# Weight sums in halves, a moved filler unit, a pinned opening and a later transpose in a two-layer decoder trunk

## The chip, the cores and the metric

The kernel runs on one core of one Trainium2 chip (trn2). The metric is the device time of one execution in microseconds (us); lower is better. Engines are named as in the profile: PE is TensorE's matmul side and PEld its weight load, DVE is VectorE, ACT is ScalarE, POOL is GpSimd, SP is SyncE, which here only issues DMAs.

## The reference

Two decoder layers over 256 tokens of width 2048, everything in float32:

```
for i in range(2):
    h = rms_norm(x, attn_norm[i])
    x = x + (diff_attention(h) if i == 0 else mla_attention(h))
    x = x + memory_cross_attention(rms_norm(x, cross_norm[i]), mem_h)   # 256 memory tokens
    h = rms_norm(x, mlp_norm[i])
    x = x + square(relu(h @ mlp_wup[i])) @ mlp_wdown[i]                 # 2048 -> 8192 -> 2048
return rms_norm(x, final_norm)
```

Differential attention takes q, k and v from one 2048 x 6144 weight, rotates a part of each q and k head by position (RoPE), and takes the difference of two softmaxes. The layers' weights are about 0.5 GB in all, and each is read once.

## The kernel before

**Precision.** A float32 product is made of three products in a shorter format: each operand is split into a high part (a cast) and a low part (the value less its high part). For a weight tile `raw` of 128 x 2048, ScalarE casts `whi <- raw` (line 195) and VectorE subtracts `wlo <- raw, whi` (line 196), in pieces of 128 x 1024; a piece is called a half below. For each 128 rows TensorE runs activation-high x weight-high, activation-high x weight-low, activation-low x weight-high: the order matters, since the second of the three is the first that needs `wlo`.

**Pipeline.** A weight unit is one `raw` tile of 1 MB, loaded by a DMA on SP's queue. There are seven raw slots (`RAWS`), and four slots each for `whi` and `wlo`, of one half each. So ScalarE may cast a half as soon as TensorE is done with the half four before it, and VectorE must then have its low part ready when TensorE gets there. `take()` hands a unit to the matmul loops and `fill()` keeps four of them issued ahead. Just before `fill()` splits one job, it calls `begin()` of the job behind it.

**Orders.** TensorE's order is the program's own. A clock kept by the program (`clock[0]`, 0.2267 us for a product of 512 columns) decides when a side task (a transpose, a softmax) is put among the matmuls. The other engines' orders are worked out by a scheduler with its own time line, except where instructions carry an order token: those with one token stay in program order on their engine. All `wlo` subtractions and weight sums carry the token "weights" (`in_turn`).

**Seven products.** In the MLP's first matrix, and in three of the four column groups of the first layer's q and k (a subclass, `Chained`), a 2 x 2 block product is made with seven instead of eight products, p1 to p7 (`class Seven`, order p1, p5, p3, p7, p2, p6, p4). Each has two items x0 and x1 of 12 matmuls. p5 and p7 need sums of weight blocks. p5's is p1's tile plus another loaded block, and p7's is p3's tile plus the same block: a VectorE add of 128 x 2048 in place, issued in `begin()` (line 836; line 915 for `Chained`, p5 only). The sums for p6, p7 of `Chained` and p4 are made by accumulating DMAs on POOL's queue (line 839).

**The MLP line.** `mlp_line` interleaves the items: x0, x1, then one ordinary unit R of 24 matmuls, then the next product. p4 of one block runs after p1 of the next. There are seven such blocks in each of the two layers. Five ordinary units are left over, and each goes as a spare unit between x0 and x1 of p3, in blocks 2 to 6.

**The opening.** The first weight unit is loaded in four pieces of 512 columns (`split_pieces(first, 4 * CH, 4)`). The first activation unit is given transposed (`xT`), and is scaled by the norm's gains and split: ScalarE line 358 makes the high part of one 128 x 256 piece, VectorE line 359 the low part. In the program, a weight cast and an activation part alternate. TensorE runs 13 warm-up products on a blank tile meanwhile.

**The first queries.** `heads_T` evacuates q from its bank (line 522), POOL rotates it (lines 533 to 538, once for each 128 tokens, t = 0 and 1), and TensorE transposes the result (`flip`, line 159) `T_ROT + given_wait` = 24 us later by the program's clock, for both t.

Of the kernel before, what the change touches and what calls it, by code (L numbers as in the profile page):

```python
# [13 lines left out]
AF = mybir.ActivationFunctionType  # L14
ALU = mybir.AluOpType
# [6 lines left out]
CH = 512  # L22
# [23 lines left out]
def trunk(ctx, tc, x, xT, mem, memT, positions, gcols, gfinal, lam_vecs, consts, W, out):  # L46
    nc = tc.nc
# [15 lines left out]
    def nm(s):  # L63
        serial[0] += 1
        return f"{s}_{serial[0]}"

    def unit():
        return units.tile([P, 2, 4, S], F32R, tag="unit", name=nm("unit"))
# [10 lines left out]
    class Task:  # L79
        def __init__(self, gen):  # L80
            self.gen = gen
            self.done = False
            self.waits = None
            self.ready = clock[0]
            self.serial = serial[0]
            side.append(self)
            self.step()
# [53 lines left out]
    def side_bank():  # L141
        while not free_banks[0]:
            yield 0.5
        free_banks[0] -= 1
        return bank()
# [15 lines left out]
    def f32(ap):  # L161
        return ap.bitcast(F32)

    def load(dst, src, queue=None):
        tc.keep_in_program_order((queue or nc.sync).dma_start(dst, src))


    def in_turn(ins):
        tc.stamp_issue_order_token(ins.ins, "weights")
        return ins  # L170

    def raw_tile():
        return wraw.tile([P, 4 * CH], F32, tag="raw", name=nm("raw"))

    def split_weights(src, width, pieces=2, loads=1, queue=None):
# [4 lines left out]
            load(raw[:, i * m : (i + 1) * m], src[:, i * m : (i + 1) * m], queue)  # L180
        return halves_of(raw, n, pieces)

    class split_pieces:
        def __init__(self, raw, n, pieces):
            self.raw, self.n, self.m, self.i = raw, n, n // pieces, 0
            self.halves = []

        def next(self):
            m, i = self.m, self.i
            at = i * m % (self.n // 2)  # L190
            if at == 0:
                self.halves.append([whalf.tile([P, 2 * CH], F32R, tag=tag, name=nm(tag)) for tag in ("whi", "wlo")])
            hi, lo = (w[:, at : at + m] for w in self.halves[-1])
            r = self.raw[:, i * m : (i + 1) * m]
            nc.scalar.copy(hi, r)  # L195
            in_turn(nc.vector.tensor_tensor(lo, r, f32(hi), ALU.subtract))  # L196
            self.i += 1

    def halves_of(raw, n=4 * CH, pieces=2):
        split = split_pieces(raw, n, pieces)  # L200
        for _ in range(pieces):
            split.next()
        return split.halves
# [135 lines left out]
    def transpose4(src, pt):  # L339

        for k in range(4):
            flip(pt[:, k * P : (k + 1) * P], src[:, k * P : (k + 1) * P])
        return pt.rearrange("p (k t) -> p k t", k=4)

    def given_unit(src, u, gcol, pieces=None):


        dst = Held(unit())
        rows = raw_tile().rearrange("p (k t) -> p k t", t=S)
        for k, n in ((0, 1), (1, 1), (2, 2)) if pieces else ((0, 2), (2, 2)):  # L350
            load(rows[:, k : k + n], src[:, 4 * u + k : 4 * u + k + n, :])
            if pieces and k == 0:
                load(g, gcols)
            for i in range(k, k + n):
                if pieces:
                    pieces.next()
                raw, hi, gain = rows[:, i], dst[:, 0, i], g[:, gcol + 4 * u + i : gcol + 4 * u + i + 1]
                nc.scalar.activation(hi, raw, AF.Copy, scale=gain)  # L358
                nc.vector.scalar_tensor_tensor(dst[:, 1, i], raw, gain, f32(hi), ALU.mult, ALU.subtract)
        return dst  # L360

# [158 lines left out]
    def evacuate(ps, scale):  # L520
        e = work.tile([P, CH], F32, tag="ev", name=nm("ev"), bufs=EVS)
        nc.scalar.activation(e[:, : ps.shape[1]], ps, AF.Copy, scale=scale)
        return e
# [16 lines left out]
    def heads_T(ps, t, scale, dst, rot=None, spare=False, given=None, given_wait=0.0):  # L540


        def task():
            while given and not given():
                yield 0.5
            e = evacuate(ps, scale() if given else scale)
            if rot:
                cos, sin, heads, half = rot
                rope(e.rearrange("p (h d) -> p h d", h=heads), cos, sin, heads, half)
            yield T_ROT + given_wait if rot else T_EV  # L550
            b = ps
            if spare:
                b = yield from side_bank()
            split(dst, t, transpose4(e, b))
            if spare:
                give_back()
            yield T_TURN

        dst.run(task())
# [245 lines left out]
    class Seven:  # L805
# [20 lines left out]
        def begin(self, p, x):  # L826
            r, other = self.raw, None
            if p in self.B:
                r[p, x] = self.fetch(*self.B[p], x)
            elif p == "p5":  # L830
                r[p, x], other = r.pop(("p1", x)), self.fetch(0, 1, x)
                r["12", x] = other
            elif p == "p7":
                r[p, x], other = r.pop(("p3", x)), r.pop(("12", x))
            if other is not None:
                in_turn(nc.vector.tensor_tensor(r[p, x], r[p, x], other, ALU.add))  # L836

        def added(self, o, block, x):
            tc.keep_in_program_order(nc.gpsimd.dma_start(o, self.source(*block, x), accum_op=ALU.add))  # L839
# [67 lines left out]
    class Chained(Seven):  # L907

        def begin(self, p, x):
            r = self.raw  # L910
            if p in self.B:
                r[p, x] = self.fetch(*self.B[p], x)
            elif p == "p5":
                r[p, x], r["p7", x] = r["p1", x], self.fetch(0, 1, x)
                in_turn(nc.vector.tensor_tensor(r[p, x], r[p, x], r["p7", x], ALU.add))  # L915

        def spent(self, p, x):
            if p == "p5":
# [3 lines left out]
    def mlp_line(l):  # L922

        def up(b, h):
            return Chunk(l, "up", [(b, h)]).items()

        def both(b):
            return [(b, 1), (b, 0)] if b else [(b, 0), (b, 1)]  # L930

        opened = {}

        def down(b):
            shut, begun = ((0, 1), (2, 3)) if b % 2 else ((2, 3), (0, 1))
            line = []
            for c in shut:
                line += opened.pop(c)[2:] if c in opened else Chunk(l, "down", both(b), c).items()
            for c in begun:
                if b == MLP_BLOCKS - 1:  # L940
                    line += Chunk(l, "down", both(b), c).items()
                else:
                    opened[c] = Chunk(l, "down", both(b) + both(b + 1), c).items()
                    line += opened[c][:2]
            return line

        first, rest = up(0, 0) + up(0, 1), []
        for b in range(MLP_BLOCKS - 1):
            rest += down(b)
        line, rest = first[:6], first[6:] + rest  # L950
        pairs = []
        held = None
        for b in SEVEN:
            by = {p: [] for p in Seven.ORDER}
            for item in Seven(f"mlp_wup{l}", 2 * b, b).items():
                by[item.u[0]].append(item)
            for p in Seven.ORDER[:-1]:
                pairs.append((p, by[p]))
                if p == "p1" and held:
                    pairs.append(("p4", held))  # L960
            held = by["p4"]
        extra = len(rest) - len(pairs) - 5
        for n, (p, (x0, x1)) in enumerate(pairs):
            line.append(x0)
            if p == "p3" and extra > 0 and n > 6:
                line.append(rest.pop(0))
                extra -= 1
            line += [x1, rest.pop(0)]
        line += rest[:2] + held + rest[2:]
        return line, down(MLP_BLOCKS - 1)  # L970
# [58 lines left out]
    acts = []  # L1029
    norm = Stream(G_ATTN)  # L1030
    pieces = split_pieces(first, 4 * CH, 4)
    ready.append(pieces.halves)
    for u in range(4):
        acts.append(given_unit(xT, u, G_ATTN, pieces if u == 0 else None))
# [237 lines left out]
    da_scales = []  # L1272
# [16 lines left out]
    def rotation(t):  # L1289
        return cos[:, t, :hd], sin[:, t, :hd], 4, hd  # L1290
# [53 lines left out]
    for i, dst in enumerate((q, k)):  # L1344
        ps = matmul_chunk(acts)
        for t in range(NT):
            heads_T(ps[t], t, lambda i=i, t=t: da_scales[i][t], dst, rotation(t), given=lambda: da_scales, given_wait=8.0 if i else 12.0, spare=True)
    v, before, copied = [], None, {}
    free_banks[0] -= 1
    for gi, line in enumerate(diff_lines):  # L1350
        o = attend_group(q, k, v, 5.0)
        nq, nk, nv = Held(unit()), Held(unit()), []
        other = value_steps(v) if gi == 0 else output_steps(before)
# [13 lines left out]
    o = attend_group(q, k, v, 0.0)  # L1367
    m = []
# [46 lines left out]
    ps = matmul_chunk(acts, LAT)  # L1415
    latent_piece(eq, 0, ps, 0, LAT)
    ps = matmul_chunk(acts, LAT)
# [3 lines left out]
    ps = matmul_chunk(acts, 320)  # L1421
# [70 lines left out]
    norm, m, mk = attention(project_q, project_kv, attend_latent, G_CROSS + 16)  # L1492
# [114 lines left out]
```

## Time and profile before

| | before |
|---|---|
| median of 3 runs | 2219.71 us (2217.9 to 2219.93) |
| the profiled execution, own time | 2220.47 us |
| its span, first to last instruction | 2218.4 us |
| PE busy | 2199.4 us (99%), 10733 matmuls |
| PEld busy | 1849.9 us (83%) |
| DVE busy | 1750.3 us (79%) |
| ACT busy | 1405.0 us (63%) |
| POOL busy | 186.2 us (8%) |
| HBM read | 499.08 MB, 226 GB/s over the span |
| mean granted TensorE clock | 0.998 |

The profiled execution's own time is its span plus 2.07 us around it, and lies 0.76 us above the median of the runs. A timeline row gives the start of a group of instructions, the time it took, the engine, the line, the operation with its tiles (out <- in), the count, and in brackets how long the engine had been idle before and what ended that. A busy PE is not PE at its peak: a matmul's recorded duration overlaps the next, so PE's pace is read from the distance between the starts of its rows.

### The profile page before, as it was taken

The numbers are of one execution on the slowest core, as the hardware profiler recorded it, in microseconds if no ns is written. First come the engines' busy times: TensorE is split into PE (matmuls) and PEld (weight loads), VectorE is DVE, ScalarE is ACT, GpSimd is POOL, SyncE is SP. The second block draws the span as 40 slices with busy tenths as digits, with TensorE's granted clock in tenths as the row PEclk, the third lists the DMA queues.
The fourth block names the chain that finished last, engine by engine and source line by source line (L and its number), as shares of the span: only waits on it lengthen the run. The fifth ranks groups of instructions, "written<-read, shape, count | busy, mean of one in ns | idle before, by whom it ended". The sixth has DMA issues, their size and how long they took to land.

```text
span 2218.4 us, 28131 instructions
## 1 busy us (share of the span) xinstructions
PE 2199.4 (99%) x10733; PEld 1849.9 (83%) x10733; DVE 1750.3 (79%) x1939; ACT 1405.0 (63%) x1889; POOL 186.2 (8%) x268
## 2 busy tenths in 40 slices
PE   9999999999999999999999999999999999999998
PEld 7888888988888888888889998898888888888886
DVE  7988877778878878888765767778887887887874
ACT  7666677566666666656645654656666666666664
POOL 1221120000000000000000410000000000000001
PEclk9999999999999999999999999999999999999999
DMA  9779797345886886886945343734688678688691
GB/s 371 201 251 278 236 294 249 123 151 218 258 274 223 260 271 222 262 269 218 294 158 195 115 152 129 270 134 152 227 264 268 229 252 266 228 252 270 226 305 57
DMA packets 75447, 503.00 MB, mean 227 GB/s; under 512 B 8625, under 2 KB 9009, under 8 KB 17201
## 3 DMA queue, kind: packets, MB, share of 16 engines
q1 hardware_dynamic: 63504, 421.51, 50.9%
q0 software_dynamic: 10656, 77.60, 17.9%
q10 hardware_dynamic: 1152, 2.10, 0.3%
q8 instruction: 84, 1.38, 0.2%
q14 instruction: 51, 0.41, 0.0%
HBM read 499.08 MB, written 2.10 MB: 226 GB/s over the span
## 4 chain that ended last, share of the span: by engine, by line
PE 93%; DVE 4%; ACT 1%; issue 1%; POOL 0%; DMA 0%; ACTq 0%; POOLq 0%; DVEq 0%
PE mm L155 62%; PE pr L155 25%; PE ax L155 3%; PE ax L159 2%; DVE raw L836 2%; DVE wlo L196 2%; ACT whi L195 1%; PE mm L159 1%; DMA raw<-in_da_wqkv_dram 0%; DVE unit L332 0%; DVE unit L494 0%; DVE unit L432 0%; POOL rs L371 0%; POOL rope L533 0%; DVE raw L915 0%
## 5 line engine op out<-in xcount | busy, mean ns | idle before, releaser
L196 DVE TENSOR_TENSOR wlo<-raw,whi 128x1024 fp32r<-128x1024 f32 (+3 forms) x998 | 1198.8, 1214 | 392.4 <-ACT whi L195 359.2
L195 ACT CAST whi<-raw 128x1024 fp32r<-128x1024 f32 (+3 forms) x998 | 1038.2, 1042 | 693.0 <-PE mm L155 466.7
L155 PE MATMUL mm<-whi,unit 128*128 128x512 f32 (+2 forms) x3904 | 1241.3, 388 | 4.3 <-ACT unit L358 3.4
L155 PEld LDWEIGHTS mm<-whi,unit 128*128 128x128 f32 x3904 | 729.9, 188 | 145.9 <-ACT unit L358 4.2
L155 PE MATMUL mm<-wlo,unit 128*128 128x512 f32 (+2 forms) x1952 | 753.7, 386 | 2.8 <-DVE wlo L196 2.3
L155 PE MATMUL pr<-whi,unit 128*128 128x512 f32 x1904 | 610.9, 390 | 0.0
L155 PEld LDWEIGHTS mm<-wlo,unit 128*128 128x128 f32 x1952 | 367.6, 188 | 76.3 <-DVE wlo L196 9.9
L155 PEld LDWEIGHTS pr<-whi,unit 128*128 128x128 f32 x1904 | 357.5, 188 | 73.5
L155 PE MATMUL pr<-wlo,unit 128*128 128x512 f32 x952 | 370.6, 389 | 0.0
L155 PEld LDWEIGHTS pr<-wlo,unit 128*128 128x128 f32 x952 | 178.8, 188 | 36.2
L839 POOL DMA_DIRECT2D raw<-in_mlp_wup_dram x56 | 49.1, 877 | 1118.7 <-DVE wlo L196 997.4
L836 DVE TENSOR_TENSOR raw<-raw,raw 128x2048 f32<-128x2048 f32 x56 | 127.9, 2284 | 0.0
L517 DVE TENSOR_TENSOR x<-x,mm 128x512 f32<-128x512 f32 x152 | 99.7, 680 | 8.0 <-PE mm L155 7.9
L155 PE MATMUL mm<-unit,whi 128*128 128x256 f32 x512 | 93.0, 284 | 0.0
L155 PEld LDWEIGHTS mm<-unit,whi 128*128 128x128 f32 x512 | 80.2, 192 | 0.4
L371 POOL TENSOR_TENSOR rs<-rs,mhalf 128x1 f32<-128x1 f32 (+1 forms) x28 | 29.3, 1051 | 553.0 <-DVE rs L370 553.0
L155 PE MATMUL mm<-unit,wlo 128*128 128x256 f32 x256 | 72.4, 283 | 0.0
L331 ACT CAST unit<-ax 128x512 fp32r<-128x512 f32 (+1 forms) x88 | 49.3, 566 | 28.5 <-PE ax L159 25.3
L332 DVE TENSOR_TENSOR unit<-ax,unit 128x512 fp32r<-128x512 f32 (+1 forms) x88 | 57.7, 661 | 3.1
L155 PEld LDWEIGHTS mm<-unit,wlo 128*128 128x128 f32 x256 | 49.1, 192 | 0.0
L365 ACT ACTIVATE junk<-x 128x512 bf16<-128x512 f32 x56 | 35.2, 628 | 9.3 <-DVE x L517 8.3
L155 PE MATMUL ax<-unit,unit 128*128 128x256 f32 (+1 forms) x240 | 36.9, 280 | 0.0
(197 smaller groups left out, 1117.6 us busy)
## 6 DMA issues: line engine op xcount, KB each, us to landing
raw<-in_mlp_wup_dram SPq DMA_DIRECT2D x128, 1024.0 KB, 5.0
raw<-in_mlp_wdown_dram SPq DMA_DIRECT2D x128, 1024.0 KB, 6.4
raw<-in_mlp_wup_dram POOLq DMA_DIRECT2D x56, 1024.0 KB, 10.7
raw<-in_da_wqkv_dram SPq DMA_DIRECT2D x45, 1024.0 KB, 10.7
raw<-in_da_wqkv_dram POOLq DMA_DIRECT2D x18, 1024.0 KB, 11.8
raw<-in_da_wo_dram SPq DMA_DIRECT2D x16, 1024.0 KB, 10.7
raw<-in_ca_wkv_dram SPq DMA_DIRECT2D x16, 1024.0 KB, 5.0
raw<-in_mla_wo_dram SPq DMA_DIRECT2D x16, 1024.0 KB, 5.5
```

The lines of the kernel that those rows point to most:

```text
L155: return nc.tensor.matmul(o, stationary, moving, start=start, stop=stop, skip_group_check=not alone)
L159: nc.tensor.transpose(o, src, ident)
L195: nc.scalar.copy(hi, r)
L196: in_turn(nc.vector.tensor_tensor(lo, r, f32(hi), ALU.subtract))
L331: nc.scalar.copy(hi, src)
L332: nc.vector.tensor_tensor(dst[:, 1, :n, t * P : (t + 1) * P], src, f32(hi), ALU.subtract)
L365: nc.scalar.activation(junk[:, : src.shape[1]], src, AF.Square, accum_out=acc)
L371: nc.gpsimd.tensor_tensor(r[:, :n], r[:, :n], mhalf.broadcast_to([P, n]), ALU.pow)
L517: nc.vector.tensor_tensor(xc, xc, ps, ALU.add)
L836: in_turn(nc.vector.tensor_tensor(r[p, x], r[p, x], other, ALU.add))
L839: tc.keep_in_program_order(nc.gpsimd.dma_start(o, self.source(*block, x), accum_op=ALU.add))
```

## The change

Four edits:

1. A weight sum is no longer issued whole in `begin()`. `sum_between` puts it on a list, `between`, as two adds of 128 x 1024, and the next two calls of `split_pieces.next()` (any unit's) each issue one of them, after the cast and ahead of the low part. All carry the token "weights".
2. The spare unit in blocks 2 to 6 of the MLP line goes between x0 and x1 of p5, no longer of p3.
3. In the opening, the four casts of the first weight unit and the four high parts of the first activation unit carry a new token, "opening", so that ScalarE runs them as the program has them, in turn.
4. The wait of the first queries' transposes is 3 us longer for t = 1.

```diff
+    def opening(ins):
+        tc.stamp_issue_order_token(ins.ins, "opening")
...
+    between = []
+
+    def sum_between(o, other, n=2):
+
+        m = 4 * CH // n
+        for i in range(n):
+            at = slice(i * m, (i + 1) * m)
+            between.append(lambda at=at: in_turn(nc.vector.tensor_tensor(o[:, at], o[:, at], other[:, at], ALU.add)))
...
             self.halves = []
+            self.placed = None
...
-            nc.scalar.copy(hi, r)
+            cast = nc.scalar.copy(hi, r)
+            if self.placed:
+                self.placed(cast)
+            if between:
+                between.pop(0)()
             in_turn(nc.vector.tensor_tensor(lo, r, f32(hi), ALU.subtract))
...
-                nc.scalar.activation(hi, raw, AF.Copy, scale=gain)
+                part = nc.scalar.activation(hi, raw, AF.Copy, scale=gain)
+                if pieces:
+                    opening(part)
...
             if other is not None:
-                in_turn(nc.vector.tensor_tensor(r[p, x], r[p, x], other, ALU.add))
+                sum_between(r[p, x], other)
...
                 r[p, x], r["p7", x] = r["p1", x], self.fetch(0, 1, x)
-                in_turn(nc.vector.tensor_tensor(r[p, x], r[p, x], r["p7", x], ALU.add))
+                sum_between(r[p, x], r["p7", x])
...
-            if p == "p3" and extra > 0 and n > 6:
+            if p == "p5" and extra > 0 and n > 6:
...
     pieces = split_pieces(first, 4 * CH, 4)
+    pieces.placed = opening
...
-            heads_T(ps[t], t, ..., given_wait=8.0 if i else 12.0, spare=True)
+            heads_T(ps[t], t, ..., given_wait=8.0 if i else 12.0 + 3.0 * t, spare=True)
```

More of the change, by code (lines that the diff above doesn't have):

```diff
@@ L1346, in trunk @@
         for t in range(NT):
-            heads_T(ps[t], t, lambda i=i, t=t: da_scales[i][t], dst, rotation(t), given=lambda: da_scales, given_wait=8.0 if i else 12.0, spare=True)
+            heads_T(ps[t], t, lambda i=i, t=t: da_scales[i][t], dst, rotation(t), given=lambda: da_scales, given_wait=8.0 if i else 12.0 + 3.0 * t, spare=True)
     v, before, copied = [], None, {}
```

## The prediction

> **What bounds the kernel now.** I read the page first, then PE's waits, then PE's timeline at each wait, and beside it the timeline of the engine that it waited for.
>
> ```profile
> span 2218.4 us, 28131 instructions
> ...
> PE 2199.4 (99%) x10733; PEld 1849.9 (83%) x10733; DVE 1750.3 (79%) x1939; ACT 1405.0 (63%) x1889; POOL 186.2 (8%) x268
> ...
> L836 DVE TENSOR_TENSOR raw<-raw,raw 128x2048 f32<-128x2048 f32 x56 | 127.9, 2284 | 0.0
> ```
>
> TensorE is the bound nearly everywhere, and the change leaves its 10733 matmuls as they are. So all that can be won is time in which PE stands still or runs slowly. What ended its waits:
>
> ```profile
> PE mm L155 <- ACT unit L358: 3.4, 2, 2.4
> PE mm L155 <- DVE wlo L196: 2.3, 12, 0.2
> PE ax L159 <- POOL ev L538: 1.3, 1, 1.3
> ```
>
> These are the three places that the change touches: the opening (line 358), the low parts (line 196, twelve times), and the rotated queries (line 538). The sums of idle time are too small, because a matmul's recorded duration runs into the wait. I therefore take distances between starts. Here is the wait for a low part in one MLP block; PE's rows, then DVE's:
>
> ```profile
> 690.70 0.39 PE L155 MATMUL mm<-whi,unit 128*128 128x512 f32 x1
> 691.28 0.50 PE L155 MATMUL mm<-wlo,unit 128*128 128x512 f32 x1 [0.19 <-DVE wlo L196]
> 691.62 0.62 PE L155 MATMUL mm<-whi,unit 128*128 128x512 f32 x2
> ```
> ```profile
> 686.07 1.23 DVE L196 TENSOR_TENSOR wlo<-raw,whi 128x1024 fp32r<-128x1024 f32 x1 [1.49 <-ACT whi L195]
> 687.21 2.28 DVE L836 TENSOR_TENSOR raw<-raw,raw 128x2048 f32<-128x2048 f32 x1
> 689.41 0.68 DVE L332 TENSOR_TENSOR unit<-ax,unit 128x512 fp32r<-128x512 f32 x1
> 690.01 2.35 DVE L196 TENSOR_TENSOR wlo<-raw,whi 128x1024 fp32r<-128x1024 f32 x2
> ```
>
> The undisturbed pace is 0.23 us between starts (a row of two takes 0.46 to the next row). Here the steps are 0.58 and 0.34, so the wait costs 0.35 + 0.11 = 0.46 us. The place is the unit R after p4: its first low part (690.01) stands behind p5's whole sum (687.21). Twelve waits are the six blocks with a p4 ahead of p5, in two layers. The list of waits leaves out weaker ones of the same kind:
>
> ```profile
> 74.01 0.39 PE L155 MATMUL mm<-whi,unit 128*128 128x512 f32 x1
> 74.53 0.50 PE L155 MATMUL mm<-wlo,unit 128*128 128x512 f32 x1
> ...
> 527.78 0.39 PE L155 MATMUL mm<-whi,unit 128*128 128x512 f32 x1
> 528.24 0.50 PE L155 MATMUL mm<-wlo,unit 128*128 128x512 f32 x1
> 528.58 0.63 PE L155 MATMUL mm<-whi,unit 128*128 128x512 f32 x2
> ...
> 1049.35 0.39 PE L155 MATMUL mm<-whi,unit 128*128 128x512 f32 x1
> 1049.81 0.50 PE L155 MATMUL mm<-wlo,unit 128*128 128x512 f32 x1
> ```
>
> Steps of 0.46 and 0.34 instead of 0.23 cost 0.34 us: at p5 of block 1 (527.78), and at p7 of block 7, the last one, which has no spare unit (1049.35). Both come in each layer. 74.01 is p5 of the first `Chained` group: 0.52 for 0.23, with the slow step behind it 0.4 us.
>
> **The change, part by part.**
>
> *Sums in halves.* In the block above, half a sum goes in at 687.21 and ends 1.14 us later (half of 2.28). Line 332's 0.6 may still come between. R's first low part then begins near 688.95 and is there at 690.2, and PE needs it at 690.70 + 0.23 = 690.93. The other half, and R's second low part, end where they ended before (about 692.3), and PE needs that part only half a unit (2.72 us) later, at 693.7. So the wait goes, with 0.7 us in hand. Gain: 12 x 0.46 = 5.5, 4 x 0.34 = 1.4, and 0.4 at 74 us. What is late next: in blocks 1 and 7, p5's second sum now lies between the low parts of p5's x0, but as much DVE work stands ahead of the second of those as before, and no PE wait showed there. Bounds for the three together: 0 if other DVE work takes the freed place, 7.3 if all goes; I take 7.3, as 0.7 us is more than the 0.6 us of the one other operation that stands there.
>
> Two instructions for one cost DVE more: two passes of 1024 columns take 2.35 (690.01) and one of 2048 takes 2.28, so 0.07 for each of 62 sums, 4.3 us in all. DVE is idle for 21% of the span, and only 0.07 of it stands ahead of any one low part, so I cost it at nothing; were all of it on the path, the gain would be 6.0 instead of 10.3. [...]
>
> *The spare unit inside p5.* No work is added. One ordinary unit (24 matmuls, 5.44 us) separates p5's x0 and x1 in ten blocks: p5's second sum gets more room, p7's less. Without the spare unit, p7's whole sum cost 0.34 us (block 7). With the half sum, R's first low part behind p3 comes 1.1 us earlier, against about 0.2 us that it was late. So nothing for p7 either; if the halves did not help, ten blocks x 0.34 = 3.4 us would be lost. The move also passes the spare unit's load ahead of two others on SP's queue, and p1's second raw tile is held longer:
>
> ```profile
> 692.39 0.33 SPq L165 DMA_DIRECT2D raw<-in_mlp_wup_dram  x1
> 697.46 2.60 SPq L165 DMA_DIRECT2D raw<-in_mlp_wdown_dram  x2
> ```
> ```profile
> raw<-in_mlp_wdown_dram SPq DMA_DIRECT2D x128, 1024.0 KB, 6.4
> ```
> ```profile
> 705.46 1.05 ACT L195 CAST whi<-raw 128x1024 fp32r<-128x1024 f32 x1 [0.81 <-PE mm L155]
> ```
>
> Each load starts when a slot comes free. The spare unit's is the first of the two at 697.46; it lands near 703.9 and is cast at 705.46: 1.6 us in hand. After the change it takes an earlier place, and the tightest load becomes that of R behind p5, which starts near 692.4, lands at 698.8, and is cast when PE is half through the spare unit, near 701.8: 3.0 us in hand. No cost, no gain.
>
> *The opening.* ACT's rows, PE's, and two windows (length, busy time of PE, PEld, DVE, ACT and POOL, then the granted clock, DMA share, GB/s):
>
> ```profile
> 5.81 0.62 ACT L195 CAST whi<-raw 128x512 fp32r<-128x512 f32 x1 [0.30 <-DMA raw<-in_da_wqkv_dram]
> 6.34 0.50 ACT L358 ACTIVATE unit<-raw,g 128x256 fp32r<-128x256 f32 x1
> 9.39 0.62 ACT L195 CAST whi<-raw 128x512 fp32r<-128x512 f32 x1 [2.55 <-DMA raw<-in_da_wqkv_dram]
> 9.91 0.50 ACT L358 ACTIVATE unit<-raw,g 128x256 fp32r<-128x256 f32 x1
> ...
> 13.24 1.98 ACT L195 CAST whi<-raw 128x1024 fp32r<-128x1024 f32 x2
> ```
> ```profile
> 7.60 0.51 PE L155 MATMUL mm<-whi,unit 128*128 128x512 f32 x1
> 10.47 0.50 PE L155 MATMUL mm<-whi,unit 128*128 128x512 f32 x1 [2.36 <-ACT unit L358]
> ...
> 14.93 0.62 PE L155 MATMUL mm<-whi,unit 128*128 128x512 f32 x2
> ```
> ```profile
> 10.40:11.40 1.00, 0.93 (x3) 0.52 (x4) 1.00 (x3) 1.00 (x4) 0.00 (x0) 1.00 1.04 424
> 11.40:14.80 3.40, 3.40 (x9) 2.62 (x9) 3.20 (x8) 3.40 (x7) 0.00 (x0) 0.51 1.04 372
> ```
>
> ACT ran the cast of the third piece (9.39) ahead of the second activation part (9.91) and waited for that piece's DMA with the part behind it. The part's own data were there earlier:
>
> ```profile
> 1.66 4.04 SPq L165 DMA_DIRECT2D raw<-in_xT_dram  x4
> ```
> ```profile
> raw<-in_xT_dram SPq DMA_DIRECT2D x1, 128.0 KB, 6.7
> ```
>
> Issued at 1.66, 6.7 us to landing: 8.4. Pinned, the part runs from 8.4 to 8.8, and ACT is back before the third piece lands at 9.39, so the pin delays no cast. PE then has 21 of the first unit's 24 products to do from 8.8 on instead of 10.47. Before, 14 had started by 14.93 (three to 7.60, eleven from 10.47), at half clock from 11.4 to 14.8 (0.51 in the row); ten more at 0.227 ended at 17.2. After: nine products to about 10.9, then the second half of the unit, held to the pace of its pieces, to about 13.8. There the next unit's weights are not ready:
>
> ```profile
> 14.31 2.36 DVE L196 TENSOR_TENSOR wlo<-raw,whi 128x1024 fp32r<-128x1024 f32 x2 [0.20 <-ACT whi L195]
> ```
>
> Its first low part ends at 15.5; by ACT's work ahead of the cast at 13.24 it can be some 0.3 earlier. PE's second product of that unit thus starts at 15.2 to 15.5 instead of 17.4: 1.9 to 2.2 us. I take 2.0. Bounds: 0 (hidden by the next unit's arrival) and 2.4. A loss is excluded, as nothing pinned waits for data later than what stands behind it.
>
> [...]
>
> *The queries' second turn.*
>
> ```profile
> 58.00 0.60 PE L159 MATMUL ax<-identr,ev 128*128 128x128 f32 x4
> 59.87 0.66 PE L159 MATMUL ax<-identr,ev 128*128 128x128 f32 x4 [1.27 <-POOL ev L538]
> ```
> ```profile
> 59.05 0.77 POOL L538 TENSOR_TENSOR ev<-rope,rope 128x64 f32<-128x64 f32 x1
> ```
>
> PE stood from 58.35 to 59.87 for POOL's last rotation, which ends at 59.82. Three more us on the program's clock put two or three groups of six products (1.36 each) ahead of the second turn: 2.7 or 4.1 us. But PE comes here 2 us earlier now, near 56, so the turn falls at 59.0 or 60.3, and POOL moves up only as far as its inputs do. Bounds: 0.3 and 1.4 us (1.52 less 0.1 for a second switch to transposes); I take 1.0. What waits behind this turn is the first attention group, which also needs k, turned later than either.
>
> **Sum.** 7.3 + 0 + 2.0 + 1.0 = 10.3 us. The profiled execution took 2220.47 (span 2218.4 and 2.07 around it), 0.76 above the runs' median of 2219.71. So 2210.2 for a like execution, 2209.4 as a median; I say 2209.5.
>
> **Rivals.**
> [...]
> - *The opening's gain is lost again.* PE comes to the queries 2 us earlier and waits there for POOL, or waits for the weights. Gain 7.3 and at most 1: 2212.
> - *The waits for low parts stay.* Other DVE work (two operations of 0.6 us) falls between half sum and low part. Against it: only line 332 stood there. Gain 3.4, at worst 0 with p7's loss: 2216 to 2219.
> - *Slower.* R's load behind p5 lands late, because p1's tile is held through the spare unit. It has 3.0 us in hand; each us beyond costs ten blocks x 1 us, so past 4.0 us of delay it eats the gain: 2221 at 4.1. For it: SP's queue always waits for slots. Against it: the least margin grows from 1.6 to 3.0.
>
> **How the numbers follow.** Chances: forecast 0.58, half clock 0.12, opening lost 0.17, low parts 0.09, slower 0.04. From no change I can tell about 0.2%, 4.4 us: under 2215.3 is faster, 0.87; same 0.09; slower 0.04. The range reaches from 2207.5 (all upper bounds, gain 11.1, and a us of the runs' spread) to 2215, which leaves out the last two rivals. The forecast's own range is 2208 to 2211.5.
>
> **What would show it.** PE's waits for line 196 gone, and block to block 0.46 us shorter; line 836 with 112 adds near 1.2 us; ACT's line 358 at 8.4 ahead of the cast at 9.39, and no 0.51 clock; no wait for line 538, or one under 1 us. I am wrong if PE waits appear behind p3 or inside p5, or ACT waits for MLP weights.

## The result, and the profile after

| | before | after | after / before |
|---|---|---|---|
| median, runs side by side | 2219.95 us (2217.9 to 2221.72, 6 runs) | 2209.53 us (2209.26 to 2211.09, 6 runs) | 0.9954 [0.9941, 0.9967] |
| the profiled execution | 2220.47 us | 2211.09 us | |

The changed kernel is 10.4 us faster; 2209.5 was forecast. Its profiled execution is the slowest of its six runs, 1.56 us above their median, and that will matter for the opening. The page's span and busy line of after, and the group of the new half sums:

```profile
span 2209.3 us, 28220 instructions
...
PE 2195.6 (99%) x10733; PEld 1851.4 (84%) x10733; DVE 1745.6 (79%) x2001; ACT 1404.9 (64%) x1889; POOL 185.6 (8%) x268
...
L193 DVE TENSOR_TENSOR raw<-raw,raw 128x1024 f32<-128x1024 f32 x124 | 151.3, 1220 | 0.0
```

TensorE has the same 10733 matmuls. Its idle time (span less busy) went from 19.0 to 13.7 us; the rest of the span's 9.1 us is recorded duration, of matmuls that ran into a wait or at the slow clock: a product that is recorded with 0.39 us at full pace has 0.50 behind a wait (before, 691.28) and 0.63 in before's slow stretch (12.01, granted clock 0.50). What ended PE's waits in after:

```profile
PE mm L155 <- ACT unit L323: 0.9, 2, 0.4
PE mm L155 <- DVE wlo L213: 0.8, 1, 0.8
PE mm L155 <- ACT whi L208: 0.7, 1, 0.7
PE pr L155 <- DVE wlo L213: 0.6, 1, 0.6
```

Lines 155 and 159 have kept their numbers; before's 195, 196, 358 and 538 are 208, 213, 375 and 557 here, and the half sums are line 193. Gone are the twelve waits for a low part, POOL's 1.3 us, and the 3.4 us for the opening's activation parts (line 358 in before). New are a wait each for a cast and a low part (both in the opening), and 0.6 us for a low part in a seven-product group (`pr`). The row at line 323 stands in every kernel of this study, under that kernel's line number.

To see where the time went, I cut each execution at four places that every kernel has: the queries' first turn (line 159), the first `pr` product, and the product that waits for line 323's unit at the cross-attention, once in each layer. These are PE's timeline rows, of after:

```profile
56.82 0.60 PE L159 MATMUL ax<-identr,ev 128*128 128x128 f32 x4
65.92 0.39 PE L155 MATMUL pr<-whi,unit 128*128 128x512 f32 x1
459.96 0.50 PE L155 MATMUL mm<-whi,unit 128*128 128x512 f32 x1 [0.44 <-ACT unit L323]
```

The mark of layer 1 is the like row at 1501.08; before has its two marks at 462.96 and 1506.79.

Stage lengths worked out from such rows (us; each kernel's one profiled execution):

| kernel | opening, to the first turn | turn to first `pr` | `pr` to layer 0's mark | layer 0's MLP, to layer 1's mark | layer 1's MLP, to the end |
|---|---|---|---|---|---|
| before | 58.00 | 10.57 | 394.39 | 1043.83 | 711.61 |
| after | 56.82 | 9.10 | 394.04 | 1041.12 | 708.22 |
| sums_only | 59.24 | 10.56 | 393.93 | 1040.47 | 708.90 |
| spare_only | 55.84 | 9.94 | 394.34 | 1045.70 | 713.58 |
| pin_only | 54.77 | 9.93 | 394.38 | 1043.87 | 711.75 |
| turn_only | 55.06 | 10.09 | 395.39 | 1043.82 | 711.64 |
| after_again | 54.49 | 9.10 | 394.05 | 1040.98 | 708.28 |
| all_but_spare | 55.86 | 9.10 | 394.05 | 1040.89 | 708.80 |
| all_but_turn | 55.28 | 10.80 | 393.92 | 1041.10 | 708.60 |
| all_but_pin | 55.60 | 9.11 | 394.05 | 1041.06 | 708.58 |
| quarters | 53.98 | 9.25 | 394.37 | 1040.94 | 708.56 |
| room | 55.28 | 9.10 | 394.05 | 1040.19 | 707.98 |
| room_quarters | 54.91 | 9.21 | 394.37 | 1040.11 | 709.10 |
| before_warm | 56.13 | 9.09 | 395.06 | 1043.98 | 711.94 |

In the four columns on the right, kernels that are alike in the part concerned agree to some 0.6 us. Two places are further apart: before_warm's second and third columns (taken up at turn_only), and layer 1's MLP in room and room_quarters (taken up there). The opening varies by some 2 us with the same code: after has 56.82, after_again 54.49. From before to after: opening -1.18, turn -1.47, attention -0.35 (the 0.4 of the first `Chained` group), the two MLP stages -2.71 and -3.39, in all -9.1.

Where the low parts stood, after (PE's rows, then DVE's, of the block whose rows the prediction shows, now some 4 us earlier):

```profile
686.57 0.39 PE L155 MATMUL pr<-whi,unit 128*128 128x512 f32 x1
686.79 0.39 PE L155 MATMUL mm<-whi,unit 128*128 128x512 f32 x1
687.02 0.39 PE L155 MATMUL mm<-wlo,unit 128*128 128x512 f32 x1
687.25 0.62 PE L155 MATMUL mm<-whi,unit 128*128 128x512 f32 x2
```
```profile
683.30 1.22 DVE L193 TENSOR_TENSOR raw<-raw,raw 128x1024 f32<-128x1024 f32 x1
684.44 0.68 DVE L349 TENSOR_TENSOR unit<-ax,unit 128x512 fp32r<-128x512 f32 x1
685.04 1.22 DVE L213 TENSOR_TENSOR wlo<-raw,whi 128x1024 fp32r<-128x1024 f32 x1
686.17 1.22 DVE L193 TENSOR_TENSOR raw<-raw,raw 128x1024 f32<-128x1024 f32 x1
687.30 2.35 DVE L213 TENSOR_TENSOR wlo<-raw,whi 128x1024 fp32r<-128x1024 f32 x2
```

PE's steps are 0.23 throughout. R's first low part starts at 685.04, behind half a sum and line 349, and is there at 686.26; PE takes it at 687.02. That is 0.76 us in hand, where 0.7 was worked out. The extra price of halving: the half sums at 683.30 and 686.17 take 1.14 and 1.13 to the next start, 2.27 together, and before's whole sum took 2.20 (687.21 to 689.41): 0.07 us, as costed, and on no path.

### The profile page after: what moved, and what is told of

The parts are those of the page before. It is cut to its first block, busy times and chain, and to the rows that moved or that the text cites. A ratio compares the mean times of both kernels' runs of the same rounds, so it can differ in the third digit from the quotient of the medians.

```text
span 2209.3 us, 28220 instructions
## 1 busy us (share of the span) xinstructions
PE 2195.6 (99%) x10733; PEld 1851.4 (84%) x10733; DVE 1745.6 (79%) x2001; ACT 1404.9 (64%) x1889; POOL 185.6 (8%) x268
## 4 chain that ended last, share of the span: by engine, by line
PE 96%; DMA 2%; issue 2%; DVE 0%; ACT 0%; POOLq 0%; ACTq 0%
PE mm L155 62%; PE pr L155 28%; PE ax L155 3%; PE ax L159 2%; DMA raw<-in_mlp_wup_dram 1%; PE mm L159 1%; DMA raw<-in_da_wqkv_dram 0%; DVE wlo L213 0%; ACT whi L208 0%; DVE x L536 0%; DVE unit L589 0%; ACT x L1536 0%; ACT unit L323 0%; ACT junk L384 0%; POOLq L1616 0%
## 5 line engine op out<-in xcount | busy, mean ns | idle before, releaser
L193 DVE TENSOR_TENSOR raw<-raw,raw 128x1024 f32<-128x1024 f32 x124 | 151.3, 1220 | 0.0
## 6 DMA issues: line engine op xcount, KB each, us to landing
raw<-in_mlp_wup_dram POOLq DMA_DIRECT2D x56, 1024.0 KB, 13.1
raw<-in_da_wqkv_dram POOLq DMA_DIRECT2D x18, 1024.0 KB, 11.4
```

Of the source, the lines that this page charges most:

```text
L193: between.append(lambda at=at: in_turn(nc.vector.tensor_tensor(o[:, at], o[:, at], other[:, at], ALU.add)))
```

## The experiments

The theory was the prediction's: the halves bring some 7 us, the pin some 2, the later turn some 1, the moved spare unit nothing, and the parts add up. The rivals: the spare unit is needed beside the halves; the pin's gain is really the clock's, or a matter of when DMAs land; the turn's gain is handed to the next wait. First each edit by itself on before (one chip; before's median there 2219.47, 30 runs), then each edit taken out of after (before 2219.06, 9 runs).

**sums_only.** Edit 1 on before.

```diff
+            if between:
+                between.pop(0)()
...
-                in_turn(nc.vector.tensor_tensor(r[p, x], r[p, x], other, ALU.add))
+                sum_between(r[p, x], other)
...
```

> The kernel before with the weight sums in halves alone. Theory (each wait is paid where its row stands): all waits of PE for line 196 at p5 and p7 go, 12 x 0.46 + 4 x 0.34 in the MLPs and 0.4 at the first Chained group, 7.3 us: about 2212.5 us; the wait for the rotated queries (1.3) and the one in the opening stay. Rival (the halves only move the wait; it needs the spare unit inside p5 to go): 3 us or less, with PE waits of the same kind left behind p4. Rival (the two instructions' extra 0.07 us counts on the path): about 3 us less gain than the theory.

Measured: 2212.45 us (2209.64 to 2214.97, 8 runs), ratio 0.997 [0.996, 0.998], 7.0 us less than before. The two MLP stages shrink by 3.36 and 2.71. What is left of PE's waits behind lines 207 (low parts), 369 (the opening's parts) and 549 (rotation):

```profile
PE mm L155 <- ACT unit L369: 2.6, 2, 2.3
PE ax L159 <- POOL ev L549: 1.3, 1, 1.3
...
PE pr L155 <- DVE wlo L207: 0.3, 1, 0.3
```

The twelve waits are gone with the spare unit still inside p3. The `pr` row is a new wait, at p6 of block 7 in layer 1, the layer that shrinks by 2.71 only; the account of the halves below comes back to it. This edit alone carries two thirds of the result. No run takes the halves out of after.

**spare_only.** Edit 2 on before.

```diff
-            if p == "p3" and extra > 0 and n > 6:
+            if p == "p5" and extra > 0 and n > 6:
```

> The kernel before with the spare unit moved into p5 alone, sums whole. Theory: the twelve waits stay, as they stand ahead of p5's first item, and p7's whole sum, now without the spare unit ahead of it, costs 0.34 us in ten more blocks: 3.4 us slower, about 2223 us. Rival (the unit gives p5 the room that it lacks): ten of the twelve waits go, 4.6 us faster, about 2215 us.

Measured: 2222.19 us (2220.55 to 2224.26, 11 runs), ratio 1.0015 [1.0006, 1.0023]: 2.7 us slower. The twelve waits stay, and a weaker one comes at p7, now without a spare unit ahead of it. The first row is of the list of waits, the others PE's timeline at p7 of one block:

```profile
PE mm L155 <- DVE wlo L196: 2.3, 12, 0.2
```
```profile
716.40 0.39 PE L155 MATMUL mm<-whi,unit 128*128 128x512 f32 x1
716.87 0.50 PE L155 MATMUL mm<-wlo,unit 128*128 128x512 f32 x1
717.20 0.62 PE L155 MATMUL mm<-whi,unit 128*128 128x512 f32 x2
```

Steps of 0.47 and 0.33 for 0.23 are 0.34 us, the figure that the prediction took from block 7. Ten blocks make 3.4; the two stages grew by 1.87 and 1.97, 3.8. The median grew by less because more of its runs than of before's have a mean clock of 0.999 (7 of 11, and 10 of 30); the table under before_warm compares runs of like clock.

**pin_only.** Edit 3 on before.

```diff
+            if self.placed:
+                self.placed(cast)
...
+                if pieces:
+                    opening(part)
...
+    pieces.placed = opening
```

> The kernel before with ScalarE's order in the opening pinned alone. Theory: PE is 1.2 us earlier at the queries' first turn where a half-clock window falls into the opening (as in the profiled run after the change), up to 2.7 us where none does, and POOL moves up with it, so the wait of 1.3 us for line 538 stays as it is: 2217 to 2218.7 us. Rival (POOL does not move up): the wait grows by what the opening gained, and the time stays at 2219.9 us.

Measured: 2218.09 us (2216.53 to 2222.48, 11 runs), ratio 0.9998 [0.9989, 1.0007]. The medians differ by 1.4 us, and the interval includes no change. Its profiled execution is its fastest run, with the clock at 1.00 where before has 0.51 (columns as in the prediction's windows):

```profile
11.40:14.80 3.40, 2.63 (x11) 1.69 (x10) 3.12 (x5) 3.33 (x6) 0.00 (x0) 1.00 1.04 406
```

**turn_only.** Edit 4 on before.

```diff
-            ... given_wait=8.0 if i else 12.0, spare=True)
+            ... given_wait=8.0 if i else 12.0 + 3.0 * t, spare=True)
```

> The kernel before with the first queries' second turn 3 us later alone. Theory: the wait for line 538 is gone and 1.5 us with it, 2218.4 us. Rival (the time is spent again behind it, where the unit after the Chained group's first product waits for its low part): the wait near 74 us grows and the gain is 0.5 us or less.

Measured: 2218.04 us (2215.61 to 2219.66, 11 runs), ratio 0.9996 [0.9987, 1.0005], 1.4 us less in the median but not told from no change. Its timeline shows part of the wait still there, and a new one behind it:

```profile
59.17 0.66 PE L159 MATMUL ax<-identr,ev 128*128 128x128 f32 x4 [0.75 <-POOL ev L538]
```
```profile
72.16 0.50 PE L155 MATMUL mm<-wlo,unit 128*128 128x512 f32 x1 [1.19 <-DVE wlo L196]
```

The stage with the turn is 0.48 shorter, the next one 1.00 longer: the low part behind p5's whole sum in the first `Chained` group, 0.3 us late in before, now ends the wait. Before_warm (below) shows the same exchange without this edit: its PE finds the second turn ready, with a stage of 9.09, and then waits 0.85 us for that low part (third column 395.06). So in this one profiled execution the turn needs the halves to be worth anything. The median fell by 1.4 us all the same, and not by the clock: 8 of the 11 runs have a mean clock of 0.998, with a median of 2218.24, where before's 18 such runs beside them have 2219.73. Why isn't shown.

**after_again.** The changed kernel once more, as the yardstick for the next three.

> The changed kernel again, for comparison on one chip with the three below: 2209.5 us, with single runs from 2207 to 2211.5 by whether a half-clock window falls into the opening.

Measured: 2209.17 us (2208.4 to 2209.86, 5 runs), ratio 0.9953 [0.994, 0.9965]. Its profiled execution took 2208.63; of the 2.5 us by which it beats after's profiled one 2.3 lie in the opening (54.49 for 56.82).

**all_but_spare.** After, with the spare unit back inside p3.

```diff
-            if p == "p5" and extra > 0 and n > 6:
+            if p == "p3" and extra > 0 and n > 6:
```

> The changed kernel with the spare unit back inside p3. Theory (the halves alone take the waits away; the move is worth nothing): as the changed kernel, 2209.5 us within 0.5, no PE wait for low parts in the MLP blocks. Rival (the move is needed beside the halves): some of the twelve waits behind p4 are back, up to 5.5 us slower.

Measured: 2209.83 us (2208.81 to 2211.28, 5 runs), ratio 0.9956 [0.9944, 0.9969]; 0.7 us more than after_again, with ranges that overlap, and MLP stages of 1040.89 and 708.80 for 1040.98 and 708.28. Beside the halves the move is worth nothing that can be measured, as costed; without them it costs 2.7 us. The opening of this profiled execution has the pin, and PE waits for an activation part all the same:

```profile
PE mm L155 <- ACT unit L375: 2.0, 1, 2.0
```

**all_but_turn.** After, with both turns 24 us behind.

```diff
-            ... given_wait=8.0 if i else 12.0 + 3.0 * t, spare=True)
+            ... given_wait=8.0 if i else 12.0, spare=True)
```

> The changed kernel with both of the first queries' turns at the same wait again. Theory: PE's wait for line 538's rotation is back, 0.7 to 1.5 us slower than the changed kernel, 2210.2 to 2211 us. Rival (as when it was the only edit: the time is spent behind it anyway): no difference.

Measured: 2211.4 us (2209.95 to 2212.8, 5 runs), ratio 0.9962 [0.9949, 0.9974]; 2.2 us more than after_again, whose slowest run is faster than this one's fastest. POOL's wait is back (line 557 is the last rotation):

```profile
57.37 0.66 PE L159 MATMUL ax<-identr,ev 128*128 128x128 f32 x4 [1.50 <-POOL ev L557]
```

The stage grows by 1.70 (10.80 for 9.10). With the halves in place nothing takes the gain away again.

**all_but_pin.** After, without the token "opening".

```diff
...
-                if pieces:
-                    opening(part)
...
-    pieces.placed = opening
```

> The changed kernel without the pinned opening. Theory (the pin saves only what the third weight piece lands late, which differs from run to run): 0.5 to 1.5 us slower in the median, 2210 to 2211 us, with a wider spread. Rival (the prediction's term, 2.0 us in every run): 2211.5 us. Rival (nothing): 2209.5 us.

Measured: 2210.2 us (2208.62 to 2212.3, 5 runs), ratio 0.9958 [0.9945, 0.9972]; 1.0 us more than after_again, ranges overlapping. In its profiled execution PE waits only 0.8 us for an activation part, without any pin (line 369 here):

```profile
PE mm L155 <- ACT unit L369: 0.8, 1, 0.8
```

So the size of the wait, 2.36 us where the prediction read it off before, depends on the execution: without the pin the longest is from 0.3 (turn_only) to 2.4 (before), with it from nothing (after, after_again) to 2.0 (all_but_spare).

The remaining runs asked what the opening's gain consists of, and about the new waits (before's median 2219.81, 15 runs, and for the last 2219.35, 9 runs).

**before_warm.** Before, with eight idle products put behind the first three, so that PE has work during its wait. They feed nothing.

```diff
+            if fill_wait:
+                for _ in range(fill_wait.pop()):
+                    nc.tensor.matmul(idle, blank[:, :P], blank, start=True, stop=True)
...
+    fill_wait = [8]
```

> The kernel before with eight more warm-up products on the blank tile behind TensorE's first three, in the wait for the second activation part; everything else as before. Theory (most runs of the kernel before lose 1.7 us to a half-clock stretch that follows this wait): the granted clock stays at 1.00 from 11.4 to 14.8, and the median falls by 0.5 to 1.5 us to 2218 to 2219, less than 1.7 because where the pieces land early the fillers are in the way. Rival (the clock does not hang on this wait): a half-clock stretch is still there, and the time is the same or up to 1 us more.

Measured: 2217.58 us (2216.52 to 2218.01, 11 runs), ratio 0.999 [0.9982, 0.9999]. The wait for the part is still there, but the idle products (line 250) fill it, and the clock stays up in the window where before has 0.51:

```profile
7.88 1.90 PE L250 MATMUL ax<-blank 128*128 128x512 bf16 x8
10.18 0.50 PE L155 MATMUL mm<-whi,unit 128*128 128x512 f32 x1 [0.40 <-ACT unit L363]
```
```profile
11.40:14.80 3.40, 3.40 (x16) 2.79 (x16) 3.17 (x8) 3.40 (x7) 0.00 (x0) 1.00 1.00 336
```

All 11 runs have a mean clock of 0.999. Of the 63 runs of before that stand beside the experiments, 21 have 0.999 (median 2218.05), 36 have 0.998 (2219.8) and 6 have 0.997 (2221.3). One slow stretch is thus worth about 1.8 us, which fits before's 3.4 us at 0.51 (1.7 us of work not done). By this, before has one in two runs of three; pin_only has 0.999 in 9 of 11, after and after_again in 10 of 11, all_but_pin in 3 of 5. The pin isn't all that decides it: spare_only, whose opening has before's code, has 0.999 in 7 of 11.

Runs of like mean clock can be compared: all_but_pin's with after_again's, the others with before's that ran beside them (the number of runs in brackets).

| kernel, mean clock | median of its runs, us | of the kernel compared | difference |
|---|---|---|---|
| sums_only, 0.998 | 2212.28 (5 runs) | 2219.73 (18) | -7.45 |
| spare_only, 0.999 | 2221.76 (7) | 2217.82 (10) | +3.94 |
| pin_only, 0.999 | 2217.74 (9) | 2217.82 (10) | -0.08 |
| turn_only, 0.998 | 2218.24 (8) | 2219.73 (18) | -1.49 |
| before_warm, 0.999 | 2217.58 (11) | 2218.33 (5) | -0.75 |
| all_but_pin, 0.999 | 2209.87 (3) | 2209.17 (5) | +0.70 |

The groups are small, and the mean clock is known to three digits only. But the pin's 1.4 us are all but gone at like clock, and spare_only's loss comes close to the 3.8 us of its stages.

**quarters.** After, with the second weight unit of the opening loaded and split in four pieces, against the new low-part wait at 14.46 (shown below).

```diff
-            ready.append(split_weights(W["da_wqkv"][u], CH, loads=2))
+            ready.append(split_weights(W["da_wqkv"][u], CH, pieces=4 if u == 1 else 2, loads=4 if u == 1 else 2))
```

> The changed kernel with the second weight unit loaded, cast and split in four pieces of 512 columns instead of two of 1024. Theory (the opening is now bound by that unit's first high and low part): PE's wait for its first low part (0.8 us, and up to 0.7 for the high part) goes down by the half piece's cast and subtraction, 0.5 + 0.6 us: 2208.2 us in the median. Rival (the unit's landing sets it, however it is cut): no difference, 2209.2 us.

Measured: 2209.09 us (2208.33 to 2210.4, 5 runs), ratio 0.9954 [0.9941, 0.9966], the ratio of after. In its profiled execution that wait is 0.23 instead of 0.76, with no gain that the runs can tell.

**room.** After, with one of the line's ordinary units put ahead of the last pair, p6 of block 7, against the new wait there.

```diff
         for n, (p, (x0, x1)) in enumerate(pairs):
+            if n == len(pairs) - 1:
+                line.append(rest.pop(0))
             line.append(x0)
```

> The changed kernel with one of the MLP line's last ordinary units moved ahead of block 7's p6. Theory (PE's new wait at p6's first low part, 0.4 to 0.8 us in each layer, is the accumulating DMA behind p7 landing late): both waits go, 1.0 to 1.4 us faster, about 2208 us. Rival (the DMAs are late because the slots' loads crowd them, and more of these then come first): the waits stay or move to p4 behind it, no gain.

Measured: 2208.41 us (2208.18 to 2209.8, 5 runs), ratio 0.9951 [0.9938, 0.9965]. The list of PE's waits has no row for `pr` left, and layer 0's MLP stage is 0.93 shorter than after's. It has the lowest median of the study, but the runs don't tell it from after's 2209.2 to 2209.5.

**room_quarters.** Both of these.

> Both of the last edits on the changed kernel: the ordinary unit ahead of block 7's p6, and the second weight unit in four pieces. Theory (the first pays about 1 us by itself, the second shortens the opening's wait only to have it back later): 2208.4 us, as with the first alone. Rival (each pays by itself): 2207.7 us or less.

Measured: 2209.03 us (2207.85 to 2209.66, 5 runs), ratio 0.9952 [0.9938, 0.9966]: no better than room alone. Its profiled execution has no wait at p6 of block 7, but one of 0.56 us for a low part of a `pr` product at 1950.97, in layer 1, whose stage is 1.1 longer than room's (709.10 for 707.98). There ACT's cast had waited 4.12 us, to 1948.61, for p6's sum in block 5, which took 19.6 us from its issue to landing. So room removes the wait at one place, and in another execution it comes at another.

## Why the prediction was right, point by point

**Halves, 7.3 us: right.** Alone they measure 7.0. Per layer the prediction has 3.44 (six waits of 0.46, two of 0.34); after's stages give 2.71 and 3.39. The 0.7 missing in layer 0 is a wait that the prediction did not have. PE's row and ACT's at p6 of block 7 in after, and the DMA behind it, issued by POOL:

```profile
1074.11 0.62 PE L155 MATMUL pr<-whi,unit 128*128 128x512 f32 x2
1075.37 0.50 PE L155 MATMUL pr<-wlo,unit 128*128 128x512 f32 x1 [0.65 <-DVE wlo L213]
```
```profile
1070.67 4.91 ACT L208 CAST whi<-raw 128x1024 fp32r<-128x1024 f32 x5 [3.38 <-DMA raw<-in_mlp_wup_dram]
```
```profile
1051.86 0.86 POOL L858 DMA_DIRECT2D raw<-in_mlp_wup_dram  x1 [1.40 <-DVE wlo L213]
```
```profile
raw<-in_mlp_wup_dram POOLq DMA_DIRECT2D x1, 1024.0 KB, 18.7
```

The accumulating DMA that makes p6's sum was issued at 1051.86 and landed 18.7 us later, at 1070.6. The same one took 14.3 in before, and 17.9 in sums_only. ACT waited 3.38 us for it, then cast five halves in a row, and the second low part of p6's x1 came 0.8 us late (1074.11 to 1075.37 is 1.26 where two products take 0.46). On DVE it stood behind two residual adds (line 536), which had come due meanwhile:

```profile
1072.90 1.28 DVE L536 TENSOR_TENSOR x<-x,mm 128x512 f32<-128x512 f32 x2
1074.09 3.49 DVE L213 TENSOR_TENSOR wlo<-raw,whi 128x1024 fp32r<-128x1024 f32 x3
```

"ACT waits for MLP weights" stood among the signs that the prediction named against itself, and it came true in every block: in after ACT waits for p6's sum seven times in each layer, in before once in all (0.7 us). ACT's list of waits over layer 0's blocks (500 to 1100 us), of after, then of all_but_spare:

```profile
ACT whi L208 <- DMA raw<-in_mlp_wup_dram: 16.9, 7, 3.4
```
```profile
ACT whi L208 <- DMA raw<-in_mlp_wup_dram: 3.8, 2, 3.0
```

Only in block 7 does it reach PE in after. Sums_only has it there too (0.35 us, in layer 1), and all_but_turn, all_but_spare and all_but_pin have it there in both layers: it comes with the halves. Room, which gives p6 more time, has no such wait of PE and gets the 0.9 us back. That the edits make the DMA slow is shown by their runs: over the 56 accumulating DMAs of the two MLPs the median from issue to landing is 10.7 us in before and in pin_only, 11.6 in spare_only, 12.1 in sums_only and 13.1 in after. By what means they do isn't settled: it runs beside the ordinary loads, and no run changed those alone.

**Spare unit, 0: right, and on the condition named.** It costs nothing that can be measured beside the halves and 2.7 us without them (3.4 was put down for that case; 3.8 by the stages). But the prediction looked for late transfers among SP's loads alone. Those kept time; the one whose margin the move used up is p6's accumulating DMA. With the spare unit in p3 ACT waits for it in blocks 1 and 7 only, which have no spare unit, and with the spare unit in p5 in all seven. At p6's second item in block 2 it takes 13.9 us in before, 15.7 in sums_only, 16.1 in spare_only and 18.2 in after. In after PE loses nothing there, but the prediction hadn't worked out that margin, and in room_quarters such a wait reached PE in block 5.

**Opening, 2.0 us: the step that was mis-sized.** The prediction took the third weight piece's landing at 9.39, the second activation part's at 8.4, and PE's wait of 2.36 with them, as fixed. All were one execution's. ACT's rows of after:

```profile
6.14 0.51 ACT L375 ACTIVATE unit<-raw,g 128x256 fp32r<-128x256 f32 x1
6.71 0.62 ACT L208 CAST whi<-raw 128x512 fp32r<-128x512 f32 x1
8.40 0.51 ACT L375 ACTIVATE unit<-raw,g 128x256 fp32r<-128x256 f32 x1 [1.06 <-DMA raw<-in_xT_dram]
```

The second part, which the prediction has at 8.4, starts at 6.14. What starts at 8.40 is the third part, and it waits for its own data: the third piece had been cast at 6.71. In the other pinned kernels the second part starts between 6.1 (after_again) and 8.5 (all_but_spare), where PE then waits 2.0 us: the pin takes the piece's DMA out of the part's way, but not the part's own. PE finished the first unit near 12.3 and then waited for the second one's weights, twice; the slow stretch came after that, not before:

```profile
13.20 0.50 PE L155 MATMUL mm<-whi,unit 128*128 128x512 f32 x1 [0.74 <-ACT whi L208]
14.46 0.51 PE L155 MATMUL mm<-wlo,unit 128*128 128x512 f32 x1 [0.76 <-DVE wlo L213]
```
```profile
11.40:14.80 3.40, 1.90 (x7) 1.04 (x6) 2.28 (x4) 2.48 (x5) 0.00 (x0) 1.00 1.04 359
14.80:18.00 3.20, 3.20 (x10) 2.49 (x9) 2.70 (x6) 2.41 (x6) 0.00 (x0) 0.57 1.05 424
```

The unit's second product, put at 15.2 to 15.5, starts at 14.46 here and at 13.76 in after_again, so this limit wasn't fixed either. After_again's opening is 3.5 us shorter than before's, over the prediction's upper bound of 2.4.

So in this one execution a half clock came all the same, to which the prediction gives 0.12 (the author's estimate: what decides the clock no row shows), and part of "lost again" held: it is the one run of six with a mean clock of 0.998, and the slowest. In the other five, and in all five of after_again, there was no such stretch by the mean clock. Over the runs the pin is worth 1.0 (all_but_pin) to 1.4 us (pin_only), and neither interval settles it by itself. Before_warm, which leaves ACT's order alone and only keeps PE at work, gains 2.2. At like clock the pin is worth 0.1 (pin_only) to 0.7 us (all_but_pin). That points to the clock kept up, rather than the shorter wait, as most of the pin's gain. How much of the fast clock is the pin's doing stays open, as spare_only has it in 7 runs of 11 without a pin.

**Turn, 1.0 us: right in kind, too small.** 1.47 by the stage and 2.2 us by all_but_turn, over the prediction's upper bound of 1.4. POOL's last rotation and PE's second turn, of after:

```profile
57.88 0.77 POOL L557 TENSOR_TENSOR ev<-rope,rope 128x64 f32<-128x64 f32 x1
```
```profile
60.01 0.60 PE L159 MATMUL ax<-identr,ev 128*128 128x128 f32 x4
```

The rotation ends at 58.65 and the turn starts at 60.01, 1.4 us in hand. The prediction let POOL move up less than PE; it moved up by as much (59.05 to 57.88, PE's first turn 58.00 to 56.82), so the whole wait was saved. The wait itself varies: without the later turn it is 1.3 in before and sums_only, 0.7 in spare_only and pin_only, and 1.5 in all_but_turn.

The sum came out because the errors cancel: 7.3 + 2.0 + 1.0 = 10.3 was said. The stages of the two profiled executions give 6.45 for the halves (0.35 + 2.71 + 3.39), 1.18 for the opening and 1.47 for the turn, 9.1. The three edits that gain, taken singly, give 7.0 + 1.4 + 1.4 = 9.8 in the medians (spare_only's loss of 2.7 goes with the halves), and all together 9.9 to 10.4. That the median came within 0.1 us of the forecast is luck: the opening alone varies by 2 us with the same code.

## What to carry to other kernels

An operation that stands whole ahead of a piece that the bounding engine needs next can be issued in parts between the pieces: what counts is the slack at that one place (here 0.76 us), and the extra cost of a second instruction (0.07 us here) matters only there. A filler moved to cover a wait is worth nothing once the wait is gone (here 0.7 us, with ranges that overlap), and costs what it covered elsewhere (here 2.7 us), so each edit of a bundle should be read by the wait that it removes, with and without the others, and by every transfer whose margin it takes, not only those of the queue that it reorders. Where a term of the sum hangs on when the first loads land, one profiled execution doesn't fix it (here the opening took 56.82 and 54.49 us with the same code): look at the spread of runs and of their mean clocks before taking a row for the rule, and compare runs of like clock.

## What the hardware showed that was not expected

- **The slow clock comes and goes with the same code.** Beside before's 0.51 in 11.4 to 14.8, sums_only's profiled execution (2214.97, the slowest of its runs) was slow for longer, with an opening of 59.24 us (0.50 from 10.4 to 11.4, and then):

```profile
11.40:14.80 3.40, 3.40 (x10) 2.70 (x9) 3.12 (x8) 3.40 (x8) 0.00 (x0) 0.50 1.03 355
```

  and spare_only's, whose opening has before's code, kept full speed (1.00), with PE busy for 0.84 of the 2.40 us before 10.4 (0.11 in before, 0.35 in sums_only):

```profile
8.00:10.40 2.40, 0.84 (x3) 0.43 (x4) 1.09 (x2) 1.59 (x4) 0.00 (x0) 1.00 0.99 374
...
11.40:14.80 3.40, 3.40 (x17) 2.72 (x15) 3.11 (x7) 3.40 (x7) 0.00 (x0) 1.00 1.03 405
```

  The 63 runs of before divide 21 to 42 by mean clock (0.999, and 0.998 or 0.997). Why one execution has the slow stretch and the next has none, no trace here shows, nor how busy PE must be, if that decides it.
- **DMAs of the first 10 us land at times that differ from execution to execution**: the third piece was cast at 9.39 in before, as soon as it was there, and at 6.71 in after, where no edit touches its load. The second activation part starts between 6.1 and 8.5 among the kernels with the pin.
- **An accumulating DMA of 1 MB** took 14.3 us in before and 18.7 us in after for the same tile. A plain load of that size takes 5.0 us from the same weights and 6.4 from the MLP's second (before's medians, 128 loads each).
